# Picking the rows of a second expert table six blocks ahead, with the rare blocks' condition moved among the dense rows

## The chip, the core and the metric

The kernel runs on one core of one Trainium2 chip. The metric is device time in microseconds (us) of one execution, from runs of the whole kernel. TensorE (PE in the profile) multiplies matrices, VectorE (DVE) and ScalarE (ACT) work element by element, GpSimd (POOL) issues the indirect transfers (those whose rows are picked by a list of indices) and SyncE (SP) issues the plain ones. The profile comes from one profiled execution.

## The reference, cut to what matters

Tokens T = 256, width D = 1024, two layers. Each layer adds a mixer (attention in layer 0, a convolution in layer 1) and then a PEER block, in which each token uses 128 experts (8 heads of 16) out of 16384:

```python
def peer(h, w_pq, sub_keys, expert_u, expert_v):
    q = (xt @ w_pq).reshape(T, PEER_HEADS, 2, PEER_HALF)
    ...
    top_s, top_i = lax.top_k(s, PEER_TOPK)
    ...
    gates = jax.nn.softmax(best_s, axis=-1)
    def chunk(args):
        xc, ec, gc = args
        u = expert_u[ec]
        act = jax.nn.gelu(jnp.einsum('cd,chkd->chk', xc, u))
        w = gc.astype(xc.dtype) * act
        return jnp.einsum('chk,chkd->cd', w, expert_v[ec])
```

So there are two tables of 16384 rows, U and V. The activation of a token with an expert is its product with a row of U; the output is the sum of rows of V, weighted by gate times activation.

## The kernel before, in words

**Precision.** A product in fp32 is made of three products of reduced-precision halves: high by high, high by low, low by high. Each block of a table (128 rows of 1024 numbers, 512 KB) is loaded into a `raw` buffer (four of them, `load_room` L103), then `split` (L118) makes two halves: ScalarE casts `hi` (L122) and VectorE subtracts to get `lo` (L128). There are three pairs of hi and lo. `raw` comes free when `lo` is made, `hi` and `lo` when the last matmul that reads them is done.

**First table (U stage).** All 128 blocks of U are multiplied with all tokens, in 64 pairs, `pi` = 0 to 63, with 48 matmuls L162 each (`s1_pair` L150). The tokens' transposed halves `xh` and `xo` stay in SBUF for that; they are read last by the last pair. From pair G0 = 22 to pair G1 = 54 the gates are put together beside it: 16 steps, two pairs apart, each for 16 tokens (`gate_bank` L1051: 48 small matmuls L1059 and L1063; VectorE makes the one-hots for them at L1046 to L1049 and multiplies the gates into the rows at L1076 and L1089). The products stand in the store tiles `st` as rows, one per expert, with 256 tokens.

**Ordering.** From pair G1 = 54 on, `order_steps` (L790), two small pieces in each pair, ranks the experts by how many tokens of each half used them, so that 96 of the 128 blocks can be formed from experts in order of use. Dense blocks 96 to 127 keep their rows as they are. For the 96 others the rows go to a DRAM tile `rows`: `send` (L631 to L646) issues on SP 8 blocks at a time for one half of the tokens (512 KB each, 24 in each layer), once the gates of that half were finished (`past[-3]`: three pairs ago). It shares SP's queue with the loads of U (L108).

**Second table.** First the 32 dense blocks (12 matmuls of 128x512 each: L146, L147, L148 in turn), loaded on SP. Beside them `pick` (L621, `rows_of` L733, transfer L736) fetches rows of `rows` in the new order, 128 KB each, two to each dense block, into 64 slots of one store tile `wr`; it is issued on POOL. Then 81 `mixed` blocks: 42 that both token halves use (12 matmuls) in turn with 39 that one half uses (6 matmuls), and at the end 3 more of 6 (`ends`). Each of these 84 needs its rows of V by the same list: `picked` (L726, transfer L729) issues that 512 KB indirect transfer on POOL into `raw`, right where the block is split. One more `pick` stands in every third block. So a layer has 84 picks of rows and 84 of V on POOL.

**The rare blocks.** The blocks for halves that the plan leaves out are done under a condition (`tc.If(self.rest_needed > 0)`, L707), after mixed block 60. With these inputs it is never taken. But every engine comes to the branch and passes it only when its own work ahead of it is finished, POOL when its transfers have landed too.

**Order of instructions.** A scheduler places the instructions of each engine, following dependences; `after` (L136) adds a dependence that only sets the order of issue, without a wait on data. Each engine then runs its list in order, and SP and POOL issue transfers in that order too.

Of the kernel before, what the change touches and what calls it, by code (L numbers as in the profile page):

```python
# [7 lines left out]
F32 = mybir.dt.float32  # L8
# [7 lines left out]
P = 128  # L16
D = 1024
KC = D // P
T = 256
NT = T // P  # L20
# [12 lines left out]
NK = 128  # L33
# [6 lines left out]
TB = 8  # L40
TQ = 4
G0 = 22
G1 = 54
OH = 3 * NK * TB
ND = 32
NI = NK - ND
NB = NI


A_END = 62  # L50
B_BEG, B_END = 20, 84
# [13 lines left out]
class Trunk:  # L65
    def __init__(self, ctx, tc, I, out):
        self.tc = tc
        self.nc = tc.nc
        self.I = I
        self.out = out  # L70
        pool = lambda name, bufs, **k: ctx.enter_context(tc.tile_pool(name=name, bufs=bufs, **k))
        self.cpool = pool("consts", 1)
        self.store = pool("store", 2)
        self.wraw = pool("wraw", 4)
        self.whl = pool("whl", 3)
        self.work = pool("work", 1)
        self.wc = pool("wc", 4)
        self.one = pool("one", 1)
        self.ps_acc = pool("ps_acc", 4, space=bass.MemoryType.PSUM)
        self.ps_h = pool("ps_h", 2, space=bass.MemoryType.PSUM)  # L80
        self.ps_m = pool("ps_m", 2, space=bass.MemoryType.PSUM)
        self.n = 0
        self.gates_last = None
        self.since = 3
        self.due = 0.0

# [19 lines left out]
    def load(self, src):  # L106
        raw = self.load_room()
        self.last_load = self.nc.sync.dma_start(raw, src)  # L108
        return raw

    def weights(self, src, pool_share=0):
# [480 lines left out]
    def peer(self, l, acc):  # L592
        nc, I = self.nc, self.I
        new = lambda: self.store_tile("st").rearrange("p (i t) -> p i t", t=T)
        st = [new()]
        sl = lambda i, n=2: st[i // HI][:, i % HI:i % HI + n, :]

        g = self.gain(2 * l + 1, st[0][:, HI - D // T:, :].rearrange("p i t -> p (i t)"))
        xT = self.norm_T(g, acc)
        U = I["u"][l]  # L600
        self.route_open(l)
        for h in range(PH):
            ps = self.s1_pair([I["wpq"][l, 2 * h], I["wpq"][l, 2 * h + 1]], xT, POOL_Q, h == 0)
            qT = self.qT[h % 2]
            nc.scalar.copy(qT, ps)
            self.route_scores(l, h, qT)
        route = self.route_steps()
        steps = 2 * (PH + 13)
        nb = T // TB
        done = 0  # L610
        past = [0] * 3
        rows = self.tc.dram_tile([NI * NK, T], F32, name=self.nm("rows"))
        out = rows.rearrange("(i j) t -> j i t", j=NK)
        sent = [0] * NT
        order = None
        mixed, ends = self.plan()
        turns = [b for _, b in mixed + ends]
        slot = lambda n: room[:, n % HI, :]
        picked = 0

        def pick(n, behind, most=HI):  # L621

            nonlocal picked
            for _ in range(min(n, min(most, len(turns)) - picked)):
                ins = self.rows_of(rows, turns[picked], slot(picked))
                self.tc.add_manual_dep(ins.ins, behind.ins.name,
                                       mybir.DependencyInfo(mybir.DependencyClass.Sync, mybir.DependencyReason.DATA),
                                       reason="pace")
                picked += 1

        def send(n, most):  # L631

            summed = past[-3]
            for t in range(NT):
                while most and summed * TB >= (t + 1) * P and min(sent[t] + 8, NI) <= n and sent[t] < n:
                    i = sent[t]
                    m = min(8, n - i)  # L640
                    to = NT if t == 0 and sent[1] == i and summed * TB >= T else t + 1
                    ts = slice(t * P, to * P)
                    nc.sync.dma_start(out[:, i:i + m, ts], sl(i, m)[:, :, ts])
                    for k in range(t, to):
                        sent[k] = i + m
                    most -= 1  # L646

        for pi in range(NK // 2):
            if pi == G0:
                for _ in route:  # L650
                    pass
                st.append(new())
                self.gates_open()
                self.one_hots(0)
                self.one_hots(1)
            due = min(max(0, pi + 1 - G0) * (nb // 2) // (G1 - G0), nb // 2) * 2
            todo = list(range(done, due))
            done = due
            if pi == G1:
                order = self.order_steps()  # L660

            def between(j):
                if j == 0:
                    for b in todo:
                        for q in range(TB // TQ):
                            self.gate_bank(b, q, 2 * pi, st)
                    if order is not None:
                        for _ in range(2):
                            next(order, None)

            ps = self.s1_pair([U[2 * pi], U[2 * pi + 1]], xT, between=between)
            for b in todo:
                if b + 2 < nb:
                    self.one_hots(b + 2)
            self.expert_rows(ps, sl(2 * pi), done * TB)
            if pi < G0:
                for _ in range((pi + 1) * steps // G0 - pi * steps // G0):
                    next(route, None)
            past.append(done)
            send(min(2 * pi - 2, NI), 1)  # L680
        for _ in order:
            pass

        room = self.store_tile("wr").rearrange("p (n t) -> p n t", t=T)
        acc = self.s2_open()
        self.begun = [[False] * 2 for _ in range(NT)]
        last = len(ends)
        for i in range(NI, NK):
            behind = self.expert_products(acc, self.weights(I["v%d" % l][i]), sl(i, 1)[:, 0, :], range(NT))
            send(NI, 1)  # L690
            if sent == [NI] * NT:
                pick(2, behind)
        prep = None
        for k, (ts, b) in enumerate(mixed):
            if k == 2:
                if l + 1 == DEPTH:
                    self.g_out = self.gain(2 * DEPTH, self.store_tile("g")[:, 0:D])
                else:
                    prep = self.conv_prep(l + 1)
            if prep is not None:  # L700
                next(prep, None)
            self.expert_products(acc, self.picked(l, b), slot(k), ts,
                                 0 in ts and not any(0 in v for v, _ in mixed[k + 1:]))
            if k % 3 == 0:
                pick(1, self.first_part, k + 1 + HI)
            if k == 3 * len(mixed) // 4:
                with self.tc.If(self.rest_needed > 0, preferred_fallthrough_block=False):  # L707
                    for b2 in range(NB):
                        ts2 = [t for t, (lo, hi) in enumerate(((0, A_END), (B_BEG, B_END))) if not lo <= b2 < hi]
                        if ts2:  # L710
                            w = self.wc.tile([P, T], F32, tag="wh", name=self.nm("wr"))
                            self.rows_of(rows, b2, w)
                            self.expert_products(acc, self.picked(l, b2), w, ts2)
        for _ in prep or ():
            pass
        ends = [(self.picked(l, b), self.row_parts(slot(len(mixed) + n), ts)) for n, (ts, b) in enumerate(ends)]
        prev = None
        for h in range(2):
            for n, (w, a) in enumerate(ends):
                mms = self.s2_mm(acc, w, a, 1, h, False, n == last - 1)  # L720
                if prev is not None:
                    self.after(mms[0], prev)
                prev = mms[-1]
        return acc

    def picked(self, l, b):  # L726

        raw = self.load_room()
        self.nc.gpsimd.indirect_dma_start(raw, None, self.I["v%d" % l].rearrange("i j d -> (i j) d"),  # L729
                                          bass.IndirectOffsetOnAxis(ap=self.expert[:, b:b + 1], axis=0))  # L730
        return self.split(raw)

    def rows_of(self, rows, b, w):  # L733

# [30 lines left out]
    def order_tables(self):  # L765
# [13 lines left out]
        nc.vector.tensor_scalar(self.later, self.iota1, row, None, op0=ALU.is_gt)  # L779
        self.expert = c.tile([P, NB], U32, name="expert")  # L780
        self.few = c.tile([P, 16], F16, name="few")
# [406 lines left out]
```

## Time and profile before

| what | value |
|---|---|
| median of 3 runs | 1780.62 us (1778.76 to 1781.29) |
| the profiled execution, its own time | 1782.4 us |
| its span | 1780.6 us |
| PE busy, share of the span | 1719.9 us, 97% |
| DVE busy | 1316.1 us, 74% |
| ACT busy | 912.6 us, 51% |
| POOL busy | 511.7 us, 29% |
| mean granted TensorE clock | 0.988 |
| U stage, last seven pairs with ordering, layer 0 and layer 1 | 539.0 to 592.2, 1425.2 to 1476.8 |
| dense blocks, layer 0 and layer 1 | 609.4 to 696.4, 1493.9 to 1581.0 |
| mixed blocks and ends, layer 0 and layer 1 | 696.4 to 887.0, 1581.0 to 1773.0 |

Positions are us from the start of the span. A row of a timeline gives the start, the length, the engine, the line and operation, the tiles written and read, the number of instructions put together, and in brackets the idle time of the engine before it and what ended that. A row of the chain of waits gives start, length and what the end of the program hung on then. "issue" is time in which an engine waited for nothing that the profile shows. A row of a table by windows gives the window, its length, the busy time of each engine with its instruction count, the granted clock, the share of the DMA engines and GB/s. PE's busy time counts slow matmuls at their full length, so 97% busy doesn't say that the matmuls ran at their best pace.

### The profile page before, as it was taken

Reading aid. Unit: us, or ns where it says so; the run is one execution under the profiler, and the core shown is the slowest. Engines: PE = TensorE matmul, PEld = TensorE weight load, DVE = VectorE, ACT = ScalarE, POOL = GpSimd, SP = SyncE. Lnnn points to the kernel's source line nnn. Section 1 sums busy time; section 2 is a strip of 40 time slices with the busy share of each in tenths; the row PEclk is TensorE's granted clock in tenths of the full one; section 3 lists DMA queues with packets and bytes.
Section 4 is the critical chain, followed back from the end, with each engine's and each line's share of the span. In section 5 each row is a group of like instructions: output and inputs, shape, how many; then the busy total and the mean of one; then the engine's idle time right before and its main releaser. Section 6 shows DMA issues by size and latency. Waiting matters only on the chain.

```text
span 1780.6 us, 32897 instructions
## 1 busy us (share of the span) xinstructions
PE 1719.9 (97%) x12606; PEld 1577.3 (89%) x12606; DVE 1316.1 (74%) x2724; ACT 912.6 (51%) x1515; POOL 511.7 (29%) x443
## 2 busy tenths in 40 slices
PE   8999999999999999998899899999999999999988
PEld 6879999999998988776798799999999989887766
DVE  4667995777897766676788689947879886666656
ACT  4653454544543455676654534554544434555545
POOL 1304000000000277765476230000000003777653
PEclk9999999999999999999999899999999999999999
DMA  7435555447648687786742355554475586878766
GB/s 270 136 135 184 178 177 190 145 154 227 206 161 271 206 288 263 254 271 227 245 142 84 106 187 178 180 184 151 155 243 184 170 266 223 289 251 261 251 218 204
DMA packets 146284, 361.13 MB, mean 203 GB/s; under 512 B 13248, under 2 KB 64704, under 8 KB 146112
## 3 DMA queue, kind: packets, MB, share of 16 engines
q1 hardware_dynamic: 113856, 248.76, 41.4%
q0 software_dynamic: 32256, 110.12, 18.9%
q8 instruction: 103, 1.69, 0.4%
q14 instruction: 69, 0.57, 0.1%
HBM read 332.61 MB, written 26.21 MB: 202 GB/s over the span
## 4 chain that ended last, share of the span: by engine, by line
PE 71%; DMA 8%; issue 4%; DVE 4%; POOL 3%; ACT 2%; SPq 1%; POOLq 0%; ACTq 0%; DVEq 0%
PE ps_h L162 47%; DMA raw<-in_v_dram,expert 8%; PE acc L147 5%; PE acc L148 5%; PE acc L146 5%; PE ps_g L1059 3%; POOL raw L729 2%; ACT hi L122 1%; PE uses L1063 1%; DVE ps_v L492 1%; DVE lo L128 1%; POOL wr L736 1%; PE ps_c L469 1%; PE ps_s L940 1%; DMA raw<-in_u_dram 1%
## 5 line engine op out<-in xcount | busy, mean ns | idle before, releaser
L122 ACT CAST hi<-raw 128x1024 fp32r<-128x1024 f32 x576 | 603.0, 1048 | 611.4 <-PE ps_h L162 388.8
L128 DVE TENSOR_TENSOR lo<-raw,hi 128x1024 fp32r<-128x1024 f32 x536 | 655.8, 1225 | 311.5 <-ACT hi L122 308.5
L162 PE MATMUL ps_h<-xh,hi 128*128 128x256 f32 x2560 | 730.4, 286 | 2.0 <-ACT hi L122 2.0
L162 PE MATMUL ps_h<-xh,lo 128*128 128x256 f32 x2560 | 724.3, 284 | 4.5 <-DVE lo L128 4.5
L162 PE MATMUL ps_h<-xo,hi 128*128 128x256 f32 x2560 | 719.6, 284 | 0.0
L162 PEld LDWEIGHTS ps_h<-xh,lo 128*128 128x128 f32 x2560 | 492.0, 192 | 6.1 <-DVE lo L128 6.1
L162 PEld LDWEIGHTS ps_h<-xh,hi 128*128 128x128 f32 x2560 | 492.5, 192 | 4.3 <-ACT hi L122 2.3
L162 PEld LDWEIGHTS ps_h<-xo,hi 128*128 128x128 f32 x2560 | 489.2, 192 | 0.2
L736 POOL DMA_INDIRECT wr<-rows,expert x168 | 186.0, 1107 | 914.3 <-ACT ps_h L1088 846.4
L147 PE MATMUL acc<-lo,wh 128*128 128x512 f32 x760 | 299.6, 394 | 2.2 <-DVE lo L128 1.5
L148 PE MATMUL acc<-hi,wl 128*128 128x512 f32 x760 | 297.2, 391 | 0.0
L146 PE MATMUL acc<-hi,wh 128*128 128x512 f32 x760 | 218.0, 395 | 21.7 <-ACT hi L122 20.8
L729 POOL DMA_INDIRECT raw<-in_v_dram,expert x168 | 189.0, 1125 | 111.7 <-issue 40.6
L146 PEld LDWEIGHTS acc<-hi,wh 128*128 128x128 f32 x760 | 142.1, 189 | 59.6 <-ACT hi L122 29.5
L147 PEld LDWEIGHTS acc<-lo,wh 128*128 128x128 f32 x760 | 143.1, 188 | 40.9 <-DVE lo L128 11.2
L148 PEld LDWEIGHTS acc<-hi,wl 128*128 128x128 f32 x760 | 143.3, 189 | 29.1
L128 POOL TENSOR_TENSOR lo<-raw,hi 128x1024 fp32r<-128x1024 f32 x40 | 95.5, 2389 | 124.0 <-ACT hi L122 116.7
L1059 PE MATMUL ps_g<-oh 128*128 128x128 f16 x1024 | 86.9, 219 | 0.0
L1076 DVE SCALAR_TENSOR_TENSOR st<-ps_g,st 128x256 f32<-128x256 f32 (+5 forms) x216 | 65.3, 340 | 24.1 <-PE ps_g L1059 24.1
L1063 PE MATMUL uses<-oh 128*128 128x96 f16 x512 | 82.9, 204 | 0.0
L1079 ACT ACTIVATE st<-ps_g 128x256 f32<-128x256 f32 (+16 forms) x168 | 42.5, 305 | 68.9 <-DVE st L1076 58.6
L741 ACT CAST wh<-wr 128x256 fp32r<-128x256 f32 (+1 forms) x168 | 58.2, 348 | 34.2 <-PE acc L147 25.9
(210 smaller groups left out, 1538.7 us busy)
## 6 DMA issues: line engine op xcount, KB each, us to landing
raw<-in_u_dram SPq DMA_DIRECT2D x256, 512.0 KB, 3.5
raw<-in_v_dram SPq DMA_DIRECT2D x64, 512.0 KB, 4.0
rows<-st SPq DMA_DIRECT2D x48, 512.0 KB, 6.8
raw<-in_wpq_dram SPq DMA_DIRECT2D x32, 512.0 KB, 4.0
raw<-in_pw_dram SPq DMA_DIRECT2D x24, 512.0 KB, 3.5
raw<-in_wqk_dram SPq DMA_DIRECT2D x16, 512.0 KB, 3.7
raw<-in_wv_dram SPq DMA_DIRECT2D x8, 512.0 KB, 6.5
raw<-in_wo_dram SPq DMA_DIRECT2D x8, 512.0 KB, 3.4
```

The source lines that it names most:

```text
L122: ins = [nc.scalar.copy(hi, raw)]
L128: ins.append(eng.tensor_tensor(lo, raw, hi.bitcast(F32), op=ALU.subtract))
L146: return [mm(ps, wh, xh, start=first, stop=False), mm(ps, wh, xo, start=False, stop=False), mm(ps, wo, xh, start=False, stop=last)]
L147: mm(ps, wh, xo, start=False, stop=False),
L148: mm(ps, wo, xh, start=False, stop=last)]
L162: mm = self.nc.tensor.matmul(ps[:, j, :], w[:, c * P:(c + 1) * P], x[:, c, :], start=n == 0, stop=n == len(terms) - 1)
L729: self.nc.gpsimd.indirect_dma_start(raw, None, self.I["v%d" % l].rearrange("i j d -> (i j) d"), bass.IndirectOffsetOnAxis(ap=self.expert[: ...
L736: return self.nc.gpsimd.indirect_dma_start(w, None, rows, at)
L741: self.first_part = self.nc.scalar.copy(hi[:, cs], w[:, cs])
L1059: mm = nc.tensor.matmul(ps[:, t, :], self.oh[:, b % 2, 0, tp, :, e], self.oh[:, b % 2, 1 + k, tp, :, e], start=k == 0, stop=k == 1)
L1063: use = nc.tensor.matmul(self.uses[:, tok // P, :], self.oh[:, b % 2, 0, tp, :, e], self.oh[:, b % 2, 1, tp, 0:NI, e], start=tok == 0, sto ...
L1076: nc.vector.scalar_tensor_tensor(v, ps[:, :, lo:lo + m].rearrange("p t i -> p i t"), 1.0 / GS, v, op0=ALU.mult, op1=ALU.mult)
```

## The change

It has five parts.

- The gates are made in 30 pairs (G1 52), still in 16 steps, so two of the steps are one pair apart and not two. Ordering begins at pair 52 with one piece to a pair, and from pair 56 has two again.
- A send now waits until its gates are five pairs old (`LAG`), and the scheduler is told to issue it after the load before it and ahead of the load behind it.
- The room for picked rows opens at the dense block in which the last sends go out, and picks begin in the one behind it: two for each dense block until 123, one for each of the last four.
- The condition for the rare blocks stands after dense block 120 and no longer after mixed block 60.
- Fetching rows of V is split from casting them. Four fetches are issued in the dense part, and then always up to six blocks ahead. Beside the four `raw` buffers, four more stand in the room of `xh` and `xo`, which the U stage no longer needs; every second fetch goes there, but for the last eight, which all go to `raw`. In mixed blocks 65 to 72 there is a pick of rows in each block.

The diff, without context that doesn't matter:

```diff
-G1 = 54
+G1 = 52
+LAG = 5
...
     def load(self, src):
         raw = self.load_room()
         self.last_load = self.nc.sync.dma_start(raw, src)
+        if self.last_send is not None:
+            self.after(self.last_load, self.last_send)
+            self.last_send = None
         return raw
...
-        past = [0] * 3
+        past = [0] * LAG
...
-            summed = past[-3]
+            summed = past[-LAG]
...
-                    nc.sync.dma_start(out[:, i:i + m, ts], sl(i, m)[:, :, ts])
+                    self.last_send = nc.sync.dma_start(out[:, i:i + m, ts], sl(i, m)[:, :, ts])
+                    self.after(self.last_send, self.last_load)
...
-                        for _ in range(2):
+                        for _ in range(1 if pi < G1 + 4 else 2):
                             next(order, None)
...
-            send(min(2 * pi - 2, NI), 1)
+            send(min(2 * (pi + 2 - LAG), NI), 1)
...
-        room = self.store_tile("wr").rearrange("p (n t) -> p n t", t=T)
+        room = None
...
-            send(NI, 1)
-            if sent == [NI] * NT:
-                pick(2, behind)
+            if room is None:
+                send(NI, 1)
+                if sent == [NI] * NT:
+                    room = self.store_tile("wr").rearrange("p (n t) -> p n t", t=T)
+                    self.last_send = None
+            else:
+                pick(2 if i < NK - 4 else 1, behind)
+            if i == NK - 8:
+                with self.tc.If(self.rest_needed > 0, preferred_fallthrough_block=False):
+                    for b2 in range(NB):
...
+                            self.expert_products(acc, self.split(self.fetch(l, b2)), w, ts2)
+
+                more = [self.one.tile([P, 2, D], F32, tag=k, name=self.nm(k)) for k in ("xh", "xo")]
+                more = [v[:, k, :] for k in range(2) for v in more]
+                there = [more[n // 2 % 4] if n % 2 and n < len(turns) - 8 else None for n in range(len(turns))]
+                raws = []
+            if i >= NK - 4:
+                raws.append(self.fetch(l, turns[len(raws)], there[len(raws)]))
...
-            self.expert_products(acc, self.picked(l, b), slot(k), ts,
+            while len(raws) < min(k + 7, len(turns)):
+                raws.append(self.fetch(l, turns[len(raws)], there[len(raws)]))
+            self.expert_products(acc, self.split(raws[k]), slot(k), ts,
                                  0 in ts and not any(0 in v for v, _ in mixed[k + 1:]))
-            if k % 3 == 0:
+            if k % 3 == 0 or picked < k + 12:
                 pick(1, self.first_part, k + 1 + HI)
-            if k == 3 * len(mixed) // 4:
-                with self.tc.If(self.rest_needed > 0, preferred_fallthrough_block=False):
...
-    def picked(self, l, b):
+    def fetch(self, l, b, raw=None):
-        raw = self.load_room()
+        raw = self.load_room() if raw is None else raw
         self.nc.gpsimd.indirect_dma_start(raw, None, self.I["v%d" % l].rearrange("i j d -> (i j) d"),
                                           bass.IndirectOffsetOnAxis(ap=self.expert[:, b:b + 1], axis=0))
-        return self.split(raw)
+        return raw
```

How the order moves is seen at two places. The first is SP's list in layer 0 near the end of the U stage, before the change: L108 is a load of a block of U, L643 a send (`st` tile to `rows`), and x8 says that eight stand in a row.

```order
L108 DMA raw_6919<-in_u_dram 128x1024
L108 DMA raw_6953<-in_u_dram 128x1024
L643 DMA rows_2057<-st_1297 128x8x128 x8
L108 DMA raw_7006<-in_u_dram 128x1024
L643 DMA rows_2057<-st_3572 128x8x128 x3
L108 DMA raw_7040<-in_u_dram 128x1024
L643 DMA rows_2057<-st_3572 128x8x128
L108 DMA raw_7092<-in_u_dram 128x1024
```

The same place after the change, where L110 is the load, L649 the send and L915 reads the register that the condition tests.

```order
L110 DMA raw_6884<-in_u_dram 128x1024
L110 DMA raw_6917<-in_u_dram 128x1024
L649 DMA rows_2057<-st_1297 128x8x128
L110 DMA raw_6951<-in_u_dram 128x1024
L110 DMA raw_7004<-in_u_dram 128x1024
L649 DMA rows_2057<-st_1297 128x8x128
L110 DMA raw_7038<-in_u_dram 128x1024
L915 TENSOR_LOAD fitu
L915 ISA x2
L110 DMA raw_7090<-in_u_dram 128x1024
L649 DMA rows_2057<-st_1297 128x8x128
```

The bunches of eight and three have become single sends with two loads between them; the last three sends stand between the first loads of V.

The second place is POOL's list around the condition in layer 0, before the change. L729 fetches rows of V, L736 picks rows, and the branches are those of L707; the line of dots stands for the body, which is not run.

```order
L729 DMA raw_9618<-in_v_dram,expert 128x1024
L736 DMA wr_7623<-rows_2057,expert 128x256
L893 TENSOR_LOAD fitu
L707 COMPARE_AND_BRANCH
L707 ISA
L707 UNCONDITIONAL_BRANCH
...
L707 UNCONDITIONAL_BRANCH
L729 DMA raw_10687<-in_v_dram,expert 128x1024
L729 DMA raw_10704<-in_v_dram,expert 128x1024
L729 DMA raw_10727<-in_v_dram,expert 128x1024
L729 DMA raw_10745<-in_v_dram,expert 128x1024
L736 DMA wr_7623<-rows_2057,expert 128x256
```

After the change L751 is a fetch of rows of V, L758 a pick, and the condition is L706. These are the rows from the first pick in layer 0 on.

```order
L758 DMA wr_7694<-rows_2057,expert 128x256 x2
L751 DMA xo_9269<-in_v_dram,expert 128x1024 x2
L751 DMA xh_9268<-in_v_dram,expert 128x1024 x2
L758 DMA wr_7694<-rows_2057,expert 128x256 x42
L915 TENSOR_LOAD fitu
L706 COMPARE_AND_BRANCH
...
L706 UNCONDITIONAL_BRANCH
L758 DMA wr_7694<-rows_2057,expert 128x256 x7
L751 DMA raw_9365<-in_v_dram,expert 128x1024
L758 DMA wr_7694<-rows_2057,expert 128x256
```

Ahead of the branch now stand 44 picks and the four fetches into the room of x, which the scheduler has put in front of most of the picks; behind it stand the other 40 picks and 80 fetches of the layer, and no branch comes among them any more. On SP 25 loads of V stand ahead of the branch and 7 behind it.

More of the change, by code (lines that the diff above doesn't have):

```diff
@@ L689, in peer @@
             behind = self.expert_products(acc, self.weights(I["v%d" % l][i]), sl(i, 1)[:, 0, :], range(NT))
-            send(NI, 1)
-            if sent == [NI] * NT:
-                pick(2, behind)
+            if room is None:
+                send(NI, 1)
+                if sent == [NI] * NT:
+                    room = self.store_tile("wr").rearrange("p (n t) -> p n t", t=T)
+                    self.last_send = None
+            else:
[3 more added lines that the diff above has]
+                    for b2 in range(NB):
+                        ts2 = [t for t, (lo, hi) in enumerate(((0, A_END), (B_BEG, B_END))) if not lo <= b2 < hi]
+                        if ts2:
+                            w = self.wc.tile([P, T], F32, tag="wh", name=self.nm("wr"))
+                            self.rows_of(rows, b2, w)
+                            self.expert_products(acc, self.split(self.fetch(l, b2)), w, ts2)
[5 more added lines that the diff above has]
+                raws.append(self.fetch(l, turns[len(raws)], there[len(raws)]))
         prep = None
@@ L701, in peer @@
                 next(prep, None)
-            self.expert_products(acc, self.picked(l, b), slot(k), ts,
+            while len(raws) < min(k + 7, len(turns)):
+                raws.append(self.fetch(l, turns[len(raws)], there[len(raws)]))
+            self.expert_products(acc, self.split(raws[k]), slot(k), ts,
                                  0 in ts and not any(0 in v for v, _ in mixed[k + 1:]))
-            if k % 3 == 0:
+            if k % 3 == 0 or picked < k + 12:
                 pick(1, self.first_part, k + 1 + HI)
-            if k == 3 * len(mixed) // 4:
-                with self.tc.If(self.rest_needed > 0, preferred_fallthrough_block=False):
[L708 to L713, printed above, removed]
         for _ in prep or ():
             pass
-        ends = [(self.picked(l, b), self.row_parts(slot(len(mixed) + n), ts)) for n, (ts, b) in enumerate(ends)]
+        ends = [(self.split(raws[len(mixed) + n]), self.row_parts(slot(len(mixed) + n), ts)) for n, (ts, b) in enumerate(ends)]
         prev = None
```

## The prediction

> **What bounds the kernel now.** I read the page first, for the engine that carries the program.
>
> ```profile
> PE 1719.9 (97%) x12606; PEld 1577.3 (89%) x12606; DVE 1316.1 (74%) x2724; ACT 912.6 (51%) x1515; POOL 511.7 (29%) x443
> PE 71%; DMA 8%; issue 4%; DVE 4%; POOL 3%; ACT 2%; SPq 1%; POOLq 0%; ACTq 0%; DVEq 0%
> ```
>
> TensorE carries 71% of the chain that ended last; transfers, issue and POOL hold 8, 4 and 3%. So time is to be had only where PE waits or runs slowly. The stages that the change touches, by windows (length, busy time of PE, its weight loads, DVE, ACT, POOL, then granted clock, DMA share, GB/s):
>
> ```profile
> 539.00:592.20 53.20, 49.52 (x445) 48.17 (x444) 42.69 (x77) 18.75 (x23) 0.00 (x0) 0.94 0.77 242
> 696.40:887.00 190.60, 179.86 (x761) 141.50 (x760) 126.90 (x171) 130.57 (x240) 116.92 (x104) 0.98 0.77 251
> 1425.20:1476.80 51.60, 47.18 (x444) 45.70 (x443) 42.57 (x76) 18.81 (x23) 0.00 (x0) 1.00 0.78 250
> 1493.90:1581.00 87.10, 87.10 (x386) 72.14 (x386) 52.91 (x64) 43.64 (x65) 64.94 (x62) 1.00 0.82 274
> 1581.00:1773.00 192.00, 178.78 (x757) 140.69 (x755) 125.77 (x169) 109.67 (x169) 120.14 (x104) 0.98 0.74 238
> ```
>
> The 32 dense blocks (row four) take 87.1 us with PE never idle: 2.72 us for 12 matmuls. The mixed stage has 756 matmuls, 63 times 12, which at that pace are 63 x 2.72 = 171.4 us. It takes 190.6 and 192.0: **19.2 and 20.6 us are lost** there. What PE waited for, in the two mixed windows (total, times, longest), and its timeline, POOL's and the chain at the longest wait in layer 1:
>
> ```profile
> PE acc L146 <- ACT hi L122: 8.9, 5, 5.6
> PE acc L146 <- ACT hi L122: 11.8, 9, 6.2
> PE acc L147 <- DVE lo L128: 0.8, 1, 0.8
> ...
> 1722.73 1.22 PE L146 MATMUL acc<-hi,wh 128*128 128x512 f32 x2 [6.17 <-ACT hi L122]
> 1727.11 0.40 PE L147 MATMUL acc<-lo,wh 128*128 128x512 f32 x1
> ...
> 1716.70 0.94 POOL L729 DMA_INDIRECT raw<-in_v_dram,expert  x1 [6.54 <-issue]
> ...
> 1699.25 13.72 DMA raw<-in_v_dram,expert
> ```
>
> The longest wait is the rare blocks' condition: POOL issued nothing for 6.54 us, the first fetch behind it started at 1716.70, and PE waited 6.17. From 1722.73 to 1727.11 ten matmuls take 4.38 us and not 10 x 0.227 = 2.27, so the slow restart costs 2.1 more: about 8 us in a layer. The Trainium skill, "TensorE: Matmul & The Clock Gate", section "HAM oscillation — how this bites in real kernels", says that idle gaps over about 3.4 us put the array at half clock; by that, the trace's 6.17 us and the slow restart agree. The rest, some 11 us a layer, are short waits for a cast whose fetch came late, and slow restarts after them.
>
> In the U stage a pair without gates takes 5.81 us, and ordering adds pieces of 0.71, by the chain:
>
> ```profile
> 554.73 6.51 DMA raw<-in_u_dram
> ...
> 571.95 0.71 PE ps_i L880 x16
> 572.66 5.81 PE ps_h L162 x48
> ```
>
> The first window of the table (pairs 54 to 60) is then worth 7 x 5.81 + 4 x 0.71 + about 0.5 of smaller pieces = 44.0 us. It took 53.2 and in layer 1 51.6: **9.2 and 7.6 us lost**. SP's queue and ScalarE show the reason:
>
> ```profile
> 535.17 11.36 SPq L643 DMA_DIRECT2D rows<-st  x8
> 546.63 1.76 SPq L108 DMA_DIRECT2D raw<-in_u_dram  x1
> 548.44 6.19 SPq L643 DMA_DIRECT2D rows<-st  x3
> ...
> 554.31 1.05 ACT L122 CAST hi<-raw 128x1024 fp32r<-128x1024 f32 x1 [7.88 <-DMA raw<-in_u_dram]
> ```
>
> Eight sends hold the queue for 11.36 us and three for 6.19, with one load between: PE's next weights come late.
>
> **The change part by part.** *Sends.* None is removed; all 24 a layer stay, one behind every two loads. Their place is the pace of a pair: 1.0 MB of loads and 0.5 MB of sends in 6.52 us (5.81 + 0.71) is 241 GB/s, which the two U windows already move (242 and 250). The bunches' loss should go. What is left: waits of ordering itself, 1.2 us now,
>
> ```profile
> PE ps_i L880 <- DVE order L866: 1.2, 2, 0.9
> ...
> 504.87:518.99 14.12, 14.12 (x147) 14.08 (x146) 12.72 (x23) 6.36 (x12) 0.00 (x0) 1.00 0.48 172
> ...
> L128 DVE TENSOR_TENSOR lo<-raw,hi 128x1024 fp32r<-128x1024 f32 x4 | 4.9, 1224 | 0.0
> L1089 DVE TENSOR_TENSOR st<-ps_h,st 128x448 f32<-128x448 f32 (+1 forms) x2 | 1.3, 641 | 0.0
> ```
>
> and the two gate steps that become one pair long. A late step of two pairs needs 12.72 us of DVE in 14.12. One pair shorter, DVE saves two subtractions (2.45) and one product (0.64), so 9.6 us; PE then needs 14.12 - 5.81 = 8.3. DVE is 1.3 us behind there, which the next step's slack of 1.4 gives back; the early short step has less DVE work. I count 0 to 1.4 a layer, 1.0. With 1.0 for a send that still delays a load (from 0 to all of the old loss), 3.2 us remain: gains of 6.0 and 4.4, **10.4 us**.
>
> *The condition.* In its new place PE must first wait for a load of V on SP, behind the branch, and that for POOL's picks. POOL's pace among dense blocks and the landings:
>
> ```profile
> 612.79 1.01 POOL L736 DMA_INDIRECT wr<-rows,expert  x1 [7.57 <-ACT wh L741]
> 615.86 0.95 POOL L736 DMA_INDIRECT wr<-rows,expert  x1 [0.31 <-issue]
> 617.11 1.16 POOL L736 DMA_INDIRECT wr<-rows,expert  x1 [0.30 <-issue]
> 618.57 0.95 POOL L736 DMA_INDIRECT wr<-rows,expert  x1 [0.31 <-issue]
> ...
> raw<-in_v_dram SPq DMA_DIRECT2D x64, 512.0 KB, 4.0
> wr<-rows,expert POOLq DMA_INDIRECT x168, 4.5
> raw<-in_v_dram,expert POOLq DMA_INDIRECT x168, 5.3
> ...
> L122 ACT CAST hi<-raw 128x1024 fp32r<-128x1024 f32 x576 | 603.0, 1048 | 611.4 <-PE ps_h L162 388.8
> ```
>
> Two picks take 618.57 - 615.86 = 2.71 us, 1.36 each. The fetches into the room of x can't start before the last U pair is done, so from the stage's start POOL has 4 fetches and 42 picks ahead of the branch: the last starts at about 45 x 1.36 = 61 to 62 us, lands 4.5 later at 66.5, the load of block 121 lands 4.0 behind that, its cast takes 1.05: 71.6. PE is done with 25 blocks at 25 x 2.72 = 68.0. A wait of 3.6, or 4.3 with 0.7 for passing the branch and issuing; I take 4.2 and 1.3 for a slow restart: **5.5** (bounds 3, a short gap at full pace, and 8.5, as much as now). By the Trainium skill's rule just named, a wait of 4.2 restarts slowly each time, at the full 2.1, and the sum would be 1.6 us longer in two layers; no run here shows a wait of that length at this place.
>
> *Fetching ahead.* A fetch no longer waits for the block in whose place it goes; eight buffers hold six ahead, so no single landing of 5.3 us is met by PE. What is late next is POOL's issue. Of 168 transfers a layer, 120 stand behind the branch, and with 7 dense blocks (19 us) about 13 of them go out before the mixed stage: 107 are left in it. Behind the last come 5.3 landing, 1.05, 1.23 for lo and 2.7 of matmuls: 10.3 us. So POOL needs 107 x interval + 10.3 against PE's 171.4, and they meet at 1.506 us. From the two mixed windows, a transfer takes POOL 116.92/104 = 1.12 and 120.14/104 = 1.16, with 0.30 between: 1.42 and 1.46. But where it had to hurry:
>
> ```profile
> 1598.93 1.23 DVE L128 TENSOR_TENSOR lo<-raw,hi 128x1024 fp32r<-128x1024 f32 x1 [1.83 <-ACT hi L122]
> ...
> 1599.13 1.82 POOL L729 DMA_INDIRECT raw<-in_v_dram,expert  x1 [0.30 <-issue]
> 1601.27 1.76 POOL L729 DMA_INDIRECT raw<-in_v_dram,expert  x1 [0.31 <-issue]
> 1607.72 0.94 POOL L729 DMA_INDIRECT raw<-in_v_dram,expert  x1 [0.76 <-DVE lo L128]
> 1628.26 0.94 POOL L729 DMA_INDIRECT raw<-in_v_dram,expert  x1 [0.30 <-issue]
> ```
>
> Those last two rows are the ends of 13 transfers without a pause: 20.54/12 = 1.71 each. A fetch of 0.94 that starts while a subtraction runs (1598.93 to 1600.16) takes 1.82. The ends are thus 1.42 (no loss) and 1.71 (107 x 1.71 + 10.3 - 171.4 = 21.9). I take 1.53, near the mean of a whole stage, since POOL may now run ahead and rest: 174.0, **2.6 us** lost. The Trainium skill, "SBUF — State Buffer", section "Who interferes with whom", speaks against this change: a DVE instruction with two SBUF inputs and a GpSimd instruction that reads SBUF shut each other out for a whole instruction, whichever began first. The trace agrees for POOL (1.82 against 0.94), not for DVE, whose subtraction keeps 1.23. By that rule alone the interval would tend to the hurried one, the first rival below.
>
> Bandwidth doesn't bind: 80 x 0.524 + 27 x 0.131 MB in 171.4 us is 265 GB/s, and the dense stage moves 274 with PE never idle. More ScalarE or DVE work there is not: the same casts, 126 of 171 us on DVE. The `lo` wait at the end of each layer, 0.8, stays.
>
> *Sum.* A layer's second table loses 5.5 + 2.6 + 0.8 = 8.9 after, 19.2 and 20.6 before: gains of 10.3 and 11.7. With 10.4 that is 32.4. The profiled execution took 1782.4, so 1750.0; the median lies 1.8 below that execution: **1748 us**.
>
> **Rivals.**
>
> *POOL is the bound* (interval 1.58 to 1.66). At 1.62 it needs 183.6, a loss of 12.2 + 6.3 = 18.5 a layer: the second table gains 2.8 in all, the sum 13.2, and the time is 1767. For it: 1.71 when hurried. Against: before, a hurried POOL was late and so in step with the subtractions it called forth; 1.42 to 1.46 over the stage.
>
> *Slower, by the same lock in step all through.* At 1.71 the layer loses 28.2 against 19.9 on average, 8.3 more, twice, less 10.4: 6.2 slower, 1787. It decides from 1.68 on (107 x 1.68 + 10.3 = 190.1, which eats 5.2 of U's gain a layer). Against: it must last for 107 transfers, and where PE stalls DVE rests and a transfer takes 0.94.
>
> *The condition stalls as before.* If POOL's early fetches start late or picks take 1.46, the last pick moves 45 x 0.10 = 4.5 us, and the wait with it: 9 us in two layers, 1757.
>
> *The U stage is not mended*: single sends of up to 6 us still delay loads, or short steps stall PE. Without the 10.4: 1758.
>
> *It does not do what it says*: fetches stand six ahead in the program but each waits in POOL's list behind a pick or a buffer. Then only the condition and U gain: about 1767; with neither, 1780.
>
> **How the numbers follow.** Forecast 0.62; POOL bound 0.15; condition 0.05; U stage 0.08; not what it says 0.05; slower 0.05. The forecast's own range is from 1738 (no POOL loss and a gap of 3: 32.4 + 5.2 + 5.0 = 42.6) to 1758; with the POOL rival to 1768. So 1738 to 1768. A measurement tells 0.2%, 3.6 us, from no change. Faster holds all but the last case and a third of the one before it: 0.93; same 0.02; slower 0.05.
>
> **What would show it.** In the profile after: sends one by one on SP and no ScalarE wait of 5 us or more for U; seven pairs in about 47 us; a PE gap of 3 to 6 us after dense block 120 and none in the mixed stage over 2; the mixed windows at about 175 us; POOL's interval near 1.5. Wrong it is if POOL runs without a pause through the mixed stage at 1.6 or more, if the gap at the condition is over 8, or if loads of U still come late.

## The result and the profile after

| | before | after |
|---|---|---|
| median of 4 runs, us | 1780.95 (1778.76 to 1783.79) | 1753.78 (1752.91 to 1756.07) |
| profiled execution, its own time | 1782.4 | 1754.41 |
| its span | 1780.6 | 1752.6 |
| U stage, from the first gate product to the first matmul of the second table, layers 0 and 1 | 291.1, 290.2 | 286.0, 285.9 |
| second-table stage, from its first matmul's start to its last one's, layers 0 and 1 | 276.8, 278.7 | 269.3, 267.1 |

The ratio is 0.9849, interval 0.9831 to 0.9866: 27 us faster. The forecast was 1748, with a range of 1738 to 1768. The two spans differ by 28.0 us: 5.1 and 4.3 in the U stages, 7.5 and 11.6 in the second table, less 0.5 elsewhere.

The page of the profile after, its first part and the chain by engine:

```profile
PE 1704.3 (97%) x12606; PEld 1577.5 (90%) x12606; DVE 1319.6 (75%) x2724; ACT 910.6 (52%) x1511; POOL 508.6 (29%) x443
PE 69%; issue 6%; POOL 5%; DVE 5%; DMA 5%; ACT 3%; POOLq 0%; SPq 0%; DVEq 0%; ACTq 0%
```

PE's instructions are the same in number; it is busy 15.6 us less, because fewer matmuls run at the slow pace. In the chain, transfers fell from 8% to 5%.

The windows after: seven pairs with ordering, then dense and mixed stages of both layers (columns as before):

```profile
542.40:587.30 44.90, 44.90 (x433) 44.64 (x434) 41.85 (x72) 18.29 (x22) 0.00 (x0) 1.00 0.81 245
...
604.50:699.10 94.60, 88.86 (x387) 73.09 (x385) 51.95 (x64) 43.88 (x66) 66.73 (x64) 0.96 0.79 273
699.10:874.20 175.10, 172.08 (x759) 141.91 (x758) 129.50 (x171) 126.47 (x239) 119.34 (x106) 1.00 0.80 265
1477.60:1572.40 94.80, 89.30 (x387) 73.42 (x386) 52.44 (x64) 43.69 (x65) 67.15 (x64) 0.96 0.79 274
1572.40:1745.00 172.60, 171.84 (x757) 141.62 (x755) 127.98 (x169) 110.07 (x169) 117.63 (x105) 1.00 0.77 256
```

The pairs with ordering take 44.9 us without any idle time of PE (53.2 and 51.6 before). The mixed stages take 175.1 and 172.6 (190.6 and 192.0 before) at full clock, against a pace of 171.4. The dense stages have grown from 87.1 to 94.6 and 94.8, at a granted clock of 0.96: the condition is there now. What PE waited for in the second table of layer 0, then of layer 1:

```profile
PE acc L151 <- ACT hi L127: 8.0, 2, 5.7
PE acc L152 <- DVE lo L133: 0.8, 1, 0.8
...
PE acc L151 <- ACT hi L127: 5.5, 1, 5.5
```

The five and nine waits for a cast in the mixed windows before have become two and one in the whole of the second table, and one of them in each layer is the condition. SP's queue in the U stage and the chain there:

```profile
551.87 2.06 SPq L110 DMA_DIRECT2D raw<-in_u_dram  x2
553.98 0.43 SPq L649 DMA_DIRECT2D rows<-st  x1
557.81 3.00 SPq L110 DMA_DIRECT2D raw<-in_u_dram  x2
560.86 0.43 SPq L649 DMA_DIRECT2D rows<-st  x1
...
554.01 0.71 PE ps_i L902 x16
554.72 5.81 PE ps_h L167 x48
560.53 0.71 PE ps_i L902 x16
```

A send holds the queue 0.43 us now (eight held it 11.36 before, 1.42 each), and a pair follows an ordering piece without a gap. The two waits that are new in U, and the last fetch of layer 0, by the timelines of PE, DVE, POOL and SP:

```profile
521.63 0.23 PE L1081 MATMUL ps_g<-oh 128*128 128x128 f16 x1 [1.67 <-ACT ps_h L1110]
...
520.89 1.29 DVE L1071 TENSOR_TENSOR oh<-oh,slot 128x1024 f16<-128x1024 f16 x2
...
859.72 1.88 POOL L751 DMA_INDIRECT raw<-in_v_dram,expert  x1 [1.20 <-DVE wl L764]
...
860.81 10.90 SPq L110 DMA_DIRECT2D raw<-in_pw_dram  x4
...
870.15 0.49 PE L151 MATMUL acc<-hi,wh 128*128 128x512 f32 x1 [2.25 <-ACT hi L127]
```

The gate products of the late short step waited 1.67 us; the one-hots they read are the first of the two at 520.89, ready about when they began. (The row names ScalarE's L1110, which ended at the same moment, but these matmuls don't read what it writes. In the earlier step of one pair, where PE waited 0.9, the profile names the one-hots, L1071.) The last fetch of layer 0 got its `raw` buffer at 859.72; the loads of the convolution's weights began a microsecond later, its cast could begin at 869.06, and PE waited 2.25. Layer 1 has no stage behind it, and no such wait.

### The profile page after: what moved, and what is told of

It is laid out like the page before. It is cut to its first block, busy times and chain, and to the rows that moved or that the text cites. A ratio compares the mean times of both kernels' runs of the same rounds, so it can differ in the third digit from the quotient of the medians.

```text
span 1752.6 us, 32933 instructions
## 1 busy us (share of the span) xinstructions
PE 1704.3 (97%) x12606; PEld 1577.5 (90%) x12606; DVE 1319.6 (75%) x2724; ACT 910.6 (52%) x1511; POOL 508.6 (29%) x443
## 4 chain that ended last, share of the span: by engine, by line
PE 69%; issue 6%; POOL 5%; DVE 5%; DMA 5%; ACT 3%; POOLq 0%; SPq 0%; DVEq 0%; ACTq 0%
PE ps_h L167 48%; PE acc L151 4%; PE acc L152 4%; PE acc L153 4%; POOL wr L758 3%; PE ps_g L1081 3%; DMA wr<-rows,expert 3%; DVE lo L133 2%; ACT hi L127 2%; PE uses L1085 1%; DVE ps_v L497 1%; DMA raw<-in_v_dram 1%; DMA raw<-in_v_dram,expert 1%; PE ps_c L474 1%; PE ps_s L962 1%
## 5 line engine op out<-in xcount | busy, mean ns | idle before, releaser
L127 ACT CAST hi<-raw 128x1024 fp32r<-128x1024 f32 x500 | 523.1, 1048 | 500.6 <-PE ps_h L167 409.3
L133 DVE TENSOR_TENSOR lo<-raw,hi 128x1024 fp32r<-128x1024 f32 x460 | 561.2, 1221 | 203.6 <-ACT hi L127 199.4
L758 POOL DMA_INDIRECT wr<-rows,expert x168 | 179.5, 1068 | 918.5 <-DMA raw<-in_v_dram 855.0
L151 PE MATMUL acc<-hi,wh 128*128 128x512 f32 x760 | 214.1, 392 | 13.5 <-ACT hi L127 13.5
L751 POOL DMA_INDIRECT raw<-in_v_dram,expert x92 | 94.2, 1024 | 45.7 <-issue 18.0
```

The lines of the kernel that those rows point to most:

```text
L127: ins = [nc.scalar.copy(hi, raw)]
L133: ins.append(eng.tensor_tensor(lo, raw, hi.bitcast(F32), op=ALU.subtract))
L151: return [mm(ps, wh, xh, start=first, stop=False), mm(ps, wh, xo, start=False, stop=False), mm(ps, wo, xh, start=False, stop=last)]
L758: return self.nc.gpsimd.indirect_dma_start(w, None, rows, at)
```

## The experiments

Twelve runs in three sets of four; sets 1 and 2 ran on one chip, set 3 on another. The kernel before took 1801.9, 1784.0 and 1799.5 in the three sets, so runs are compared within a set, or by their ratio to the kernel before; the U stages were the same to 0.1 us in all sets, and what differed was the second table. That the ratio carries over from set to set is an assumption; the changed kernel, with 0.9849, 0.9850 and 0.9844, supports it.

| run | set | median, us | ratio to before, interval | second-table stages |
|---|---|---|---|---|
| sends only | 1 | 1791.7 | 0.9946 (0.9926 to 0.9967) | 287.4, 288.4 |
| condition back | 1 | 1768.9 | 0.9829 (0.9808 to 0.9850) | 270.8, 278.5 |
| four buffers | 1 | 1793.3 | 0.9947 (0.9932 to 0.9962) | 291.6, 284.2 |
| no condition | 1 | 1760.2 | 0.9786 (0.9764 to 0.9809) | 275.5, 266.1 |
| the changed kernel | 2 | 1755.9 | 0.9850 (0.9824 to 0.9877) | 269.4, 267.6 |
| no condition, few picks | 2 | 1738.4 | 0.9752 (0.9726 to 0.9778) | 262.6, 259.3 |
| extra picks | 2 | 1800.6 | 1.0111 (1.0082 to 1.0140) | 291.3, 285.9 |
| gate steps and ends | 2 | 1748.2 | 0.9808 (0.9782 to 0.9834) | 268.1, 267.6 |
| condition early | 3 | 1782.1 | 0.9914 (0.9887 to 0.9941) | 286.2, 283.7 |
| condition back again | 3 | 1771.0 | 0.9852 (0.9810 to 0.9895) | 278.5, 275.8 |
| no condition again | 3 | 1766.4 | 0.9801 (0.9778 to 0.9824) | 279.6, 273.7 |
| the changed kernel, third | 3 | 1773.0 | 0.9844 (0.9828 to 0.9860) | not used: its profiled run was 17 us over its median |

**Which part brings what.** My theory A had three separate savings: the sends, the depth of the fetches, and hardly anything from the condition's place. Theory B had the condition's place as the cause: out of the mixed stage, POOL's drain no longer sets off the short waits.

*Sends only:* the kernel before with the edits of the gates, the ordering and the sends.

```diff
-G1 = 54
+G1 = 52
+LAG = 5
...
-            summed = past[-3]
+            summed = past[-LAG]
...
+                    self.after(self.last_send, self.last_load)
...
```

> The kernel before with the change's first two parts alone: gates in 30 pairs, ordering from pair 52, sends five pairs late and one behind every two loads. Theory A (three separate savings: sends, depth of the fetches, hardly the condition's place): the U stages, counted from the first gate product to the first dense block, were 5.1 and 4.3 us shorter in the changed kernel, so 9.4 us of 1781: 1771 to 1772, and the mixed stages stay at 190 to 192 us. Theory B (the condition's place decides, the sends matter little by themselves): the same or less, 1771 to 1778.

The ratio is 0.9946, which is 9.6 us of 1781 (5.9 to 13.2 by the interval), and the U stages are 286.0 and 285.9, those of the changed kernel. The sends, with the gates and the ordering moved for them, do by themselves what they do in the whole.

*Four buffers:* the changed kernel without the room of x, fetching where a block is split.

```diff
-            while len(raws) < min(k + 7, len(turns)):
-                raws.append(self.fetch(l, turns[len(raws)], there[len(raws)]))
+            while len(raws) < k + 1:
+                raws.append(self.fetch(l, turns[len(raws)]))
...
```

> The changed kernel without its last part: no room of x, each fetch of V into one of the four raw buffers and placed where the block is split, as before; the condition stays among the dense blocks. Theory A: the short waits for late fetches (some 11 us a layer before) come back with the depth gone: 1754 + 16 to 22 = 1770 to 1776. Theory B: the depth does little once the condition is out of the way: 1754 to 1759.

0.9947: the same as the sends alone, in the same set. The two second-table stages together take 575.8 us here and 575.9 there. So moving the condition out of the mixed stage, without depth, gave nothing. Theory B fell here. PE's waits in the second table of layer 0 from 680 us on show why, as a row of eight short waits for casts beside the condition's:

```profile
PE acc L151 <- ACT hi L127: 7.5, 8, 2.1
PE acc L151 <- issue: 6.1, 2, 5.8
```

From 0.9947 to the changed kernel's 0.9849 are 17 us: what the depth is worth. This goes across sets. Within the first set there is the next run, which has the depth and differs in the condition's place: it was 24 us faster than the one with four buffers. The four more buffers and the fetching ahead were not separated.

*Condition back:* the changed kernel with the condition after mixed block 60, its body fetching into the room of x.

```diff
-                with self.tc.If(self.rest_needed > 0, preferred_fallthrough_block=False):
...
+            if k == 60:
+                with self.tc.If(self.rest_needed > 0, preferred_fallthrough_block=False):
...
+                            self.expert_products(acc, self.split(self.fetch(l, b2, more[1])), w, ts2)
```

> The changed kernel with only the condition put back behind mixed block 60; its body, which is not run, fetches into a quarter of the room of x. Theory A: six fetches have landed when PE comes to the branch, so PE waits only for ScalarE's first casts behind it, 1 to 2 us at full pace, in place of 5.5 to 5.75 and a slow restart of 1.3 to 2.1; POOL's pause of some 7 us is covered by six blocks (about 12 us). 4 to 5 us less in each layer: 1744 to 1747; no more than 1754. Theory B: a drain of POOL in the middle of the mixed stage sets off the short waits that follow, whatever the depth: 10 us or more come back in each layer, 1770 to 1776.

In the first set there was no changed kernel beside it, so it was repeated with one.

> The changed kernel with the condition back behind mixed block 60, once more, now beside the changed kernel itself. Theory A (place matters little, depth covers the drain): within 5 us of the changed kernel, or up to 10 less. Theory P (POOL's rate is the limit, so its pause costs the same wherever it stands, and six blocks of cover are not won back): 8 to 15 us more than the changed kernel, with PE waiting in the stretch behind the branch.

Ratios of 0.9829 and 0.9852 against 0.9844 to 0.9850 for the changed kernel; in the third set 1771.0 against 1773.0. The place can't be told apart, and both sets are far from what theory B wanted (a return of 10 us a layer). Neither the gain of 8 to 10 us that theory A expected of the first run nor the loss of 8 to 15 us that theory P expected of the second came. The wait at the branch is 3.7 us and not 1 to 2: ScalarE's casts begin only when PE has come to the branch, and PE starts behind a cast of picked rows that follows the second cast of a block, at 830.59 (second run, layer 0, waits of PE, then ScalarE and PE):

```profile
PE acc L151 <- ACT wh L763: 3.7, 1, 3.7
PE acc L152 <- DVE lo L133: 1.3, 2, 0.8
PE acc L151 <- ACT hi L127: 1.1, 1, 1.1
...
828.46 1.04 ACT L127 CAST hi<-xh 128x1024 fp32r<-128x1024 f32 x1 [5.88 <-PEq L729]
...
831.52 0.40 ACT L763 CAST wh<-wr 128x256 fp32r<-128x256 f32 x1
...
831.99 1.22 PE L151 MATMUL acc<-hi,wh 128*128 128x512 f32 x2 [3.71 <-ACT wh L763]
```

**What the condition costs.** *No condition:* condition and body are left out.

> The changed kernel without the condition and the rare blocks' code behind it, so the part for rare blocks is left out (it is not run with these inputs). It prices the condition in its new place. Both theories: PE's wait (5.75 and 5.5) and the slow matmuls behind it (1.3 and 2.1) go: 14.5 us less, 1739, or less of a gain if POOL, with nothing to wait for, comes to its limit later in the mixed stage: up to 1745.

> The changed kernel without the condition and its body, once more, now beside the changed kernel. Theory A (the condition's wait and its slow restart are all it costs): 14.5 us less than the changed kernel. Theory P (what PE doesn't wait at the branch it waits later for POOL): 0 to 7 us less, with waits for fetches in the last third of the mixed stage.

By ratio 0.9786 and 0.9801 against 0.9849 and 0.9844: 11 and 8 us, and 6.7 us between the medians of the third set. The wait and the slow matmuls in its place are 7.5 + 7.7 us in the trace. So between a quarter and somewhat over half of it comes back. The first run's interval reaches the 14.5 of theory A; the second lies near the upper end of the 0 to 7 of theory P (POOL's rate of issue is the next limit). The trace has short waits for fetches, as theory P has it; layer 0 of the second run, from 690 us on:

```profile
PE acc L151 <- ACT hi L127: 3.2, 3, 1.9
PE acc L152 <- DVE lo L133: 2.9, 6, 0.8
```

These waits alone don't show POOL as their cause: in the profile of the changed kernel from that set (1790 us) PE waits no less, 9.4 us from 699 on. The next two runs test it.

**Is POOL the next limit?** *No condition, few picks:* the 30 picks of rows of each layer's mixed stage go as well, and their blocks use rows of other blocks, so that part of the result is left out.

```diff
-        slot = lambda n: room[:, n % HI, :]
+        slot = lambda n: room[:, n % 54, :]
...
-            if k % 3 == 0 or picked < k + 12:
-                pick(1, self.first_part, k + 1 + HI)
```

> The changed kernel without the condition and its body, and without the last 30 picks of rows of each layer, whose blocks then use rows of other blocks (that part of the result is left out). Theory P (POOL's rate of issue is the limit left once the condition is gone): with 30 x 1.45 = 43 us less POOL work a layer PE never waits for a fetch: second-table stages of 259 to 262 in both layers, 10 to 18 us below the changed kernel beside it. Theory L (landing times or the load on the DMA engines set the limit): the stages stay above 264, and the time within 8 us of the run without the condition.

The second-table stages, dense and mixed together (95 x 2.72 = 258.4 us at PE's pace), in both layers:

```profile
605.30:867.90 262.60, 260.23 (x1142) 214.78 (x1141) 182.09 (x234) 170.43 (x304) 173.71 (x141) 0.99 0.79 260
1471.60:1730.90 259.30, 258.54 (x1142) 213.66 (x1140) 180.16 (x233) 153.86 (x233) 158.68 (x139) 1.00 0.78 255
```

Layer 1 runs at PE's pace, layer 0 within 4 us of it, and the time is 17.5 us below the changed kernel's: theory P. The DMA engines' share is 0.78 and 0.79 beside 0.77 to 0.80, which speaks against them as the limit. By ratio, 6 to 9 us of the 17.5 are the picks' part; the run without the condition stood in other sets.

*Extra picks:* 25 picks a layer are done twice.

```diff
+            if k % 3 == 1 and picked > k + 9:
+                ins = self.rows_of(rows, turns[k + 9], slot(k + 9))
...
```

> The changed kernel with 25 picks in each layer's mixed stage done a second time into the same slots (132 transfers on POOL in that stage instead of 107). Theory P: POOL then needs 132 x 1.45 + 10.3 = 202 us or more against PE's 171.4, so 20 to 35 us more in each layer, 40 to 70 in all; by the hurried interval of 1.71, 65 a layer. If POOL had room to spare: within 5 us of the changed kernel.

44.7 us more than the changed kernel. Its mixed stages, and POOL's timeline in that of layer 1:

```profile
699.50:896.50 197.00, 185.16 (x760) 140.76 (x759) 127.98 (x170) 128.07 (x239) 145.05 (x130) 0.98 0.79 251
1595.00:1786.30 191.30, 178.40 (x754) 142.29 (x753) 126.86 (x169) 109.72 (x168) 140.53 (x130) 0.98 0.77 248
...
1595.53 0.94 POOL L756 DMA_INDIRECT xh<-in_v_dram,expert  x1 [0.30 <-issue]
...
1770.55 0.94 POOL L756 DMA_INDIRECT raw<-in_v_dram,expert  x1 [0.30 <-issue]
...
1776.00 0.93 POOL L756 DMA_INDIRECT raw<-in_v_dram,expert  x1 [1.57 <-DVE wl L769]
```

POOL is the bound here. The first two rows are the ends of 126 transfers without a pause: 175.02/125 = 1.40 us each. In layer 0, too, 126 stand in a row, from 699.62 to 877.53: 1.42 each. The third row is the stage's last transfer; 10.3 us behind it, the landing and work that the prediction puts there, is 1786.3, where the stage ends. (In layer 0 the last starts at 884.72, and the stage ends 11.8 us later.) Bound by POOL, the interval is 1.40 to 1.42, not 1.71.

**Mending what the profile after shows.** *Gate steps and ends:* gates in 32 pairs, and x's room used up to the last four fetches.

```diff
-G0 = 22
-G1 = 52
-LAG = 5
+G0 = 21
+G1 = 53
+LAG = 4
...
-                there = [more[n // 2 % 4] if n % 2 and n < len(turns) - 8 else None for n in range(len(turns))]
+                there = [more[n // 2 % 4] if n % 2 and n < len(turns) - 4 else None for n in range(len(turns))]
```

> The changed kernel with the gates in 32 pairs from pair 21 to 53, so that every step is two pairs long again, sends four pairs late, and the room of x used for fetches up to the last four. If the short gate steps cost their 0.9 + 1.7 us by DVE's one-hots, and the last fetch of layer 0 came late for want of a raw buffer: 2 x 2.6 us from U and 2 to 3 at the end of layer 0, 5 to 8 less than the changed kernel beside it. If the gates' waits come from elsewhere: 0 to 3 less.

7.7 us less than the changed kernel, 0.9808 of the kernel before. The gate products start a pair (5.8 us) earlier and the U stages are 288.8 from there, so 3.0 shorter each; no wait of PE is left in them. In the second table of layer 0 PE waits only at the branch and at the very end:

```profile
PE acc L151 <- ACT hi L127: 6.0, 1, 6.0
PE acc L152 <- DVE lo L133: 0.8, 1, 0.8
```

*Condition early:* from that kernel, the condition after the third dense block, and the first fetches made to wait for block 99.

```diff
-            if i == NK - 8:
+            if i == NI + 2:
...
+            if i == NI + 3:
+                begun = behind
```

> The run with the gate steps and ends mended, and with the condition right behind the third dense block, ahead of all picks and fetches (the first fetches are made to wait for dense block 99). POOL then has nothing under way when it comes to the branch, and SP's loads behind it wait for ScalarE only: a PE wait of 2.5 to 4 us at the branch in place of 5.5 to 6, and POOL loses no time amid its list, but begins 8 us later. Second-table stages of 262 to 267 in place of 268, 2 to 10 us less in all than the run with gate steps and ends mended: 1738 to 1746. If POOL's late start counts in full: 1750 to 1756.

It lost: 1782.1 against 1773.0 for the changed kernel in its set, although it has the mended gates, and neither of the two forecasts held. POOL's first transfer and PE's wait at the branch in layer 0, whose second table begins at 600.8:

```profile
610.02 1.17 POOL L764 DMA_INDIRECT wr<-rows,expert  x1 [433.24 <-ACT wh L769]
...
614.01 2.07 PE L151 MATMUL acc<-hi,wh 128*128 128x512 f32 x4 [4.87 <-ACT hi L127]
```

The wait at the branch is hardly shorter, and POOL starts 9.2 us behind the stage's start, where the changed kernel's POOL starts before it. By ratio it is 19 us behind the kernel it was made from (0.9914 against 0.9808), about twice those 9.2 us; that the late start is the whole reason was not tested.

*The changed kernel* stood beside the others in sets 2 and 3:

> The changed kernel itself, as the measure for the runs beside it on the same chip. All theories: U stages 286.0 and 285.9 as before; second-table stages between 267 and 276, by how POOL and the slow restarts fall out on this chip; a ratio to the kernel before of 0.980 to 0.988.

> The changed kernel, as the measure for the three runs beside it: 1752 to 1757, U stages 286.0 and 285.9, second-table stages 267 to 270.

Its ratio holds, 0.9850 and 0.9844; its time in the third set, 1773, does not. Why kernels with this second table lose some 8 to 10 us a layer there in some sets (the kernel before 1801.9 against 1781, the changed one 1773 against 1756), and none in U, stays open. It is not the chip alone, since the kernel before took 1801.9 and 1784.0 on the same one. Nor is it POOL's rate alone: in the profile of the changed kernel from the third set (1790 us) PE also waits among the dense blocks, whose rows of V SP loads, for 4.1 us in layer 0 and 2.6 in layer 1 ahead of the branch, and in the second set for none.

## Why the prediction was right

The direction and the range were right, and the mechanism in the main. The sum was 32.4 us and the spans give 28.0. Some of its errors cancel each other (see "Against the sum"), and so far the agreement is luck.

- **Sends.** Forecast 6.0 and 4.4, measured 5.1 and 4.3. That bunches on SP's queue cost that time was right, as the run with the sends alone shows. The rest was put together wrongly, and it is luck that the errors nearly cancel: 1.0 for sends that still delay loads and 1.2 for the order's own waits were both 0, but the short gate steps cost 0.9 + 1.7 = 2.6 a layer, not 1.0. The loss before was put too high as well: with every step two pairs long the U stage takes 288.8 - 5.8 = 283.0 us, so 8.1 and 7.2 were lost before, not 9.2 and 7.6. The step that failed is that the next step's slack "gives back" DVE's lag: PE needs the one-hots at the start of the step, so the lag is a wait there, and slack behind it comes too late. The early step was not free either.
- **The condition.** Forecast 5.5 a layer (4.2 and 1.3), measured 94.6 - 87.1 = 7.5 and 7.7: waits of 5.75 and 5.50, and slow matmuls for 1.8 and 2.2. Up to ScalarE's first cast the chain was the one forecast, link by link. Layer 0's timelines of POOL, SP, ScalarE and PE:

```profile
668.00 0.95 POOL L758 DMA_INDIRECT wr<-rows,expert  x1 [0.30 <-issue]
...
671.64 2.65 SPq L110 DMA_DIRECT2D raw<-in_v_dram  x4
...
675.57 1.04 ACT L127 CAST hi<-raw 128x1024 fp32r<-128x1024 f32 x1 [1.40 <-DMA raw<-in_v_dram]
676.85 1.04 ACT L127 CAST hi<-raw 128x1024 fp32r<-128x1024 f32 x1 [0.24 <-DMA raw<-in_v_dram]
...
678.42 2.08 PE L151 MATMUL acc<-hi,wh 128*128 128x512 f32 x4 [5.75 <-ACT hi L127]
```

  The last pick started 63.5 us into the stage (forecast 61 to 62), SP issued the load 3.6 later, and the first cast ended at 676.61, 3.9 behind PE's last matmul: that is about the 4.2. PE began only at 678.42, 0.5 behind the second cast, though its first matmuls read only the first. Those 1.8 us I can't explain, but they are regular: in layer 1, in the changed kernel's repeat in set 2 and in the run with the mended gate steps PE again began 0.3 to 0.6 behind the second cast. The restart was slow at the full price, 1.8 and 2.2. The Trainium skill, "TensorE: Matmul & The Clock Gate", section "HAM oscillation — how this bites in real kernels", has half clock after idle gaps of over some 3.4 us; these two waits agree. The traces also have a slow restart behind a shorter wait: one of 2.05 us in layer 1 of the changed kernel's profile from the third set was followed by four matmuls in 2.07 us, as here, while behind the 2.25 us at the end of layer 0 there was none.
- **Depth.** No single landing is met by PE: right, and worth 17 us by the run with four buffers. POOL's shortage was forecast at 2.6 a layer with an interval of 1.53. Measured: 172.6 against 171.4 + 0.8 in layer 1, so 0.4, and 175.1 in layer 0, of which 2.25 is the last fetch, so 0.7. The step that failed is the interval's upper end: 1.71 came from a stretch before, and under a real shortage POOL takes 1.40 to 1.42. From start to start its transfers stood 1.54 and 1.56 us apart in the two mixed stages, close to 1.53, but for another reason: POOL waited for buffers. In the mixed stage of layer 1, POOL's own groups after:

```profile
L751 POOL DMA_INDIRECT raw<-in_v_dram,expert x41 | 41.2, 1006 | 20.6 <-DVE lo L133 10.2 <-DVE wl L764 6.4 <-issue 4.0
L758 POOL DMA_INDIRECT wr<-rows,expert x29 | 33.5, 1156 | 9.9 <-ACT wh L763 5.6 <-ACT hi L127 3.0 <-issue 1.2
L751 POOL DMA_INDIRECT xh<-in_v_dram,expert x17 | 21.2, 1249 | 8.6 <-DVE wl L764 4.5 <-issue 3.3 <-DVE lo L133 0.8
L751 POOL DMA_INDIRECT xo<-in_v_dram,expert x17 | 21.1, 1240 | 7.0 <-DVE wl L764 3.3 <-DVE lo L133 2.1 <-issue 1.5
```

  104 transfers take 117.0 us, 1.125 each, and sit idle 46.1 in front, of which 104 x 0.30 = 31 are the usual pauses: 15 us are waits for a buffer. POOL had room to spare in that run. How much is not measured; 25 more transfers a layer were too many.
- **The end of layer 0** was not in the sum: five of the eight last fetches wait for a `raw` buffer in turn, and the last one meets the loads of the next stage. The wait of 2.25 us is over the 2 that the prediction gave as a sign. It is mended by four more fetches in x's room.
- **Against the sum:** U 1.0 less, the condition 4.2 less, POOL and ends 1.9 more. Of the 1.1 us left, 0.5 is in stages outside and the rest lies in the bounds of windows.
- **The rivals.** POOL as the bound is what the kernel meets next, not what it met. The slower rival's lock in step was not seen even with 25 more transfers. That the condition stalls as before is near the truth: 7.5 against some 8. It was no worse a place, and no better. The other two fell with 5.1 and 4.3 us gained in U and mixed stages of 175.1 and 172.6.

## What to carry over

A gain from running ahead is worth what the waits for single transfers were, and is bounded by the rate of the engine that issues them: count that engine's instructions behind the last stop, times its interval, before and after. An interval taken from a hurried stretch may hold a coupling of that stretch; doubling some of the instructions on purpose measures it. When work is put into fewer, closer steps, ask what must be ready as each begins: later slack doesn't repay it.

## What was not expected of the hardware

- An indirect transfer's issue took POOL 1.12 and 1.09 us on average in the two layers when POOL was the bound (129 and 128 transfers), and 1.13 and 1.125 in the changed kernel, where it was not.
- What lengthens an issue is seen in the kernel before, in the mixed stage of layer 1: the 67 that began while VectorE ran one of its two subtractions (`lo` or `wl`) took 1.28 us on average and up to 1.99, the 35 others 0.93 to 0.95. The `lo` subtractions took 1.21 to 1.30 all the same. With the extra picks, in the same stage, it was 1.18 for 79 and 0.93 to 0.96 for the 49 others. In the stretch with 1.71 between starts an issue took 1.41 on average; why subtractions lengthened it so much more there is not shown.
- The same program took 1756 us in one set of runs and 1773 in another, with U stages equal to 0.1 us. The second-table stage is what varied.
